# A hybrid decoder layer: transposes of rotated q and k and of gated q and k by VectorE squares and GpSimd transfers

## The chip, the cores and the metric

The kernel runs on one core of a Trainium2 chip. A core has five engines that work side by side, each through its own instructions in order: TensorE (PE; its weight loads are listed apart as PEld), VectorE (DVE), ScalarE (ACT), GpSimd (POOL) and SyncE (SP), which here only issues transfers. They meet through semaphores. Operands lie in SBUF, 128 partitions wide; TensorE writes to PSUM, eight banks of 128 x 512 float32; sixteen DMA engines move data between HBM and SBUF, and from SBUF to SBUF. The metric is the device time of one execution in microseconds (us).

## The reference

One decoder layer over 256 tokens of width 2048, all in float32:

```
x = x + 1/2 * SwiGLU_1(RMSNorm(x))
h = RMSNorm(x);  z = h @ W_in
    group A: 4 heads of chunked gated linear attention (dk 128, dv 256, chunks of 64), low-rank forget gate
    group B: 8 heads of dilated causal attention (d 128), per-head RMS norm of q and k, then rotary
x = x + concat(o_A, o_B) @ W_out
x = x + 1/2 * SwiGLU_2(RMSNorm(x))
```

The change lies in the middle part. In group B, q and k are normed per head, multiplied by the cosines and sines of their position, and then multiplied with each other per head: scores = q k^T, summed over the 128 features of a head. In group A,

```
log_a = log_sigmoid(g_low @ gate_up + bias) / 16
b     = cumsum(log_a) in each chunk of 64
scores  = (q * exp(b - b_ref)) @ (k * exp(b_ref - b))^T
q_inter = q * exp(b);   k_state = k * exp(b_last - b)
```

TensorE sums over the partition dimension. A projection leaves its results with tokens on the partitions and features along the rows, so q and k must be transposed before their scores can be made: to features on the partitions, tokens along the rows.

## The kernel before

**Weights and products.** A large product streams its weights from HBM in 1 MB blocks (raw, three buffers, issued by SyncE). Each half block is split into a high part of reduced precision (wh, ScalarE, line 113) and the rest (wl, VectorE, line 114); both have four buffers. A product of float32 precision is then three matmuls of 128 x 512 (lines 274, 276, 278): high by high, high by low, low by high. `weights()` keeps two pairs prepared beyond the one in use: the split of pair i + 2 is put in the program just before the products of pair i.

**The queue of later work.** `later` is a list of small pieces of work. `column_pair` (line 366) makes 1024 output columns out of 16 pairs, each for two blocks of 128 tokens (t = 0, 1), which gives 32 half-pair steps. Before each step it takes entries from `later`, spread over `span` steps (28 where nothing is said); with `due=i` it empties the list before pair i. An entry `lambda: None` does nothing and spaces the rest out. This fixes the order in the program. The framework then orders each engine's instructions by a simulated timeline, so that what is not ready in the simulation can fall behind what comes later in the program.

**The middle part** (from line 544) runs column pairs one after the other: q of group B (into xq), k of group B (xk), v of group B (va), the low-rank gate (`gate_low`), q and k of group A (qg, kg), v of group A (vg), the output gate, and then the output projection. The work of one column pair's results lies in `later` beside the products of the next.

`rotate` (line 600) handles 128 tokens of four heads of group B: `head_scale` sums squares on ScalarE and takes the power -1/2 on GpSimd (line 165), five VectorE operations scale and rotate (lines 604 to 610) into m1, then four 128 x 128 transposes on TensorE (line 109, through an identity) fill a PSUM bank, and ScalarE copies it into qT or kT (line 614). There are eight such calls, four for q and four for k. `scores` (line 643) multiplies qT by kT, `values` (line 661) applies the probabilities to va. Both put small matmuls among the large ones; all small matmuls share two PSUM banks (tp).

`gate_low` (line 694) has its own weights: two buffers of wh are filled with zeros by GpSimd (line 203) and 16 columns of each k tile are split into them. Two matmuls of the gate's second factor follow (line 708), and for each t ScalarE takes an exponential and a logarithm (lines 712, 713). `decays` (line 718) makes the cumulative sums with TensorE and the exponentials e1, e2, e3. `scaled` (line 734) transposes qg and kg with four TensorE transposes each and VectorE multiplies the bank into e1 and e3, or e2 (line 740). `intra` and `gla_head` make the group's outputs.

**The other way to transpose** is already in the kernel, in the feed-forward parts and in half of the norms: `squares` (line 126) transposes the sixteen 32 x 32 squares of each 128 x 128 block on VectorE, all in place within their 32 partitions, and `move_squares` (line 130) carries the squares to their partitions with 16 GpSimd DMAs, each from 32 partitions to 32 others, in runs of 128 elements (512 bytes). What lands is right up to an order of 32-element runs along the rows; `in_order` and `runs` are views that put this right for the reader.

Tiles of 8 KB per partition in the middle part (xq, qT, xk, kT, va, vg, on, ogh, ogl) share four buffers under the tag `big`.

Of the kernel before, what the change touches and what calls it, by code (L numbers as in the profile page):

```python
# [21 lines left out]
P = 128  # L22
# [5 lines left out]
NT = S // P  # L28
# [20 lines left out]
def layer_kernel(tc, x, xT, gains, gla_gate_up, gla_gate_bias, gla_out_norm, att_q_norm, att_k_norm,  # L49
# [6 lines left out]
    with ExitStack() as es:  # L56
# [69 lines left out]
        def squares(dst, src):  # L126

            nc.vector.transpose(dst.rearrange("p (q j c) -> p j q c", q=4, j=4), src)

        def move_squares(dst, src):  # L130
            for q in range(4):
                for r in range(4):
                    nc.gpsimd.dma_start(dst[32 * q:32 * q + 32, r * P:(r + 1) * P], src[32 * r:32 * r + 32, q * P:(q + 1) * P])  # L133
# [59 lines left out]
        def prepare():  # L193
# [3 lines left out]
            if job == "low":  # L197
# [3 lines left out]
                for i in range(2):  # L201
                    w = wtile("wh").rearrange("p j f -> p (j f)").rearrange("p (k f) -> p k f", f=P)
                    nc.gpsimd.memset(w.bitcast(F32), 0.0)
# [340 lines left out]
        with tc.tile_pool(name="mix", bufs=1, reuse_waits="tile") as mp:  # L544
# [55 lines left out]
            def rotate(i, dst, t, half, xn):  # L600
                rs = head_scale(xn, 4, HD)
# [9 lines left out]
                tb = tp_bank()  # L611
                for h in range(4):
                    transpose(tb[:, h * P:(h + 1) * P], m1[:, h * P:(h + 1) * P])
                nc.scalar.activation(dst[:, 4 * half:4 * half + 4, t * P:(t + 1) * P], v(tb), AF.Copy)

            def store(dst, after=None):

                def f(t, ps):
                    for j in range(2):
                        blk = dst[:, t, j * 512:(j + 1) * 512]  # L620
                        nc.scalar.activation(halves(blk), ps[j], AF.Copy, scale=rt[:, t:t + 1])
                        if after:
                            later.append(lambda blk=blk, j=j: after(t, j, blk))
# [4 lines left out]


            xq, qT = big("xq"), big("qT")  # L630
            qTv = qT.rearrange("p (h s) -> p h s", h=AH)
            column_pair(hacts, store(tok(xq), lambda t, j, b: rotate(0, qTv, t, j, b)), span=14, due=8)
            xk, kT = big("xk"), big("kT")
            kTv = kT.rearrange("p (h s) -> p h s", h=AH)
            column_pair(hacts, store(tok(xk), lambda t, j, b: rotate(1, kTv, t, j, b)))
# [7 lines left out]
            def scores(h):  # L643
                b = tp_bank()
                for t in range(NT):
                    nc.tensor.matmul(b[:, t * P:t * P + (t + 1) * P], lhsT=qTv[:, h, t * P:(t + 1) * P],
                                     rhs=kTv[:, h, :(t + 1) * P], start=True, stop=True)
# [40 lines left out]
            def t4k(name):  # L688
                return mp.tile([P, NT, 512], F32, name=name, tag=name, bufs=1)

            qg, kg, la, e1, e2, e3 = (t4k(n) for n in ("qg", "kg", "la", "e1", "e2", "e3"))
            dec = mp.tile([P, NT, 8], F32, name="dec")

            def gate_low():
# [11 lines left out]
                for t in range(NT):  # L706
                    b = tp_bank()
                    nc.tensor.matmul(b, lhsT=gl[:, t * P:(t + 1) * P], rhs=gup, start=True, stop=True)
                    lg, ab = t512("lg"), t512("ab")
                    nc.vector.scalar_tensor_tensor(lg, b, rt[:, t:t + 1], gbias, op0=ALU.mult, op1=ALU.add)  # L710
                    nc.vector.scalar_tensor_tensor(ab, lg, -1.0, lg, op0=ALU.mult, op1=ALU.min)
                    nc.scalar.activation(ab, ab, AF.Exp)
# [208 lines left out]
```

## Time and profile before

| | |
|---|---|
| time, median of 3 runs (lowest to highest) | 1736.27 us (1733.95 to 1739.5) |
| profiled execution, its time | 1733.12 us |
| profiled execution, span from first to last instruction | 1731.3 us |
| mean granted TensorE clock | 0.999 |
| HBM read, written | 354.57 MB, 4.19 MB |
| rate over the span | 207 GB/s |
| transposes of the kernel on TensorE (line 109) | 120 |
| DMAs of `move_squares` (line 133) | 832 |

The profile is of one execution. A page gives each engine's busy time; the trace behind it can be asked for groups of instructions, single instructions, waits and stretches. A row of the timeline has start, length, engine, line, operation, output <- inputs by the program's names, the shape, a count, and in brackets the idle time of that engine before it with what ended it. A row of a group has a count, the busy time of all, the mean length in ns, and the idle time before them with what ended most of it. The middle part covers about 676 to 1045 us of the span.

### The profile page before, as it was taken

To read this page: it belongs to the slowest core of one execution; us is meant where nothing else is said; L and a number is where in the kernel's file an instruction comes from. 1 tells how busy PE (TensorE), PEld (TensorE's weight loads), DVE (VectorE), ACT (ScalarE), POOL (GpSimd) and SP (SyncE) were. 2 spreads that over 40 slices of the span, in tenths; PEclk is the share of its full clock that TensorE was granted. 3 is DMA by queue.
4 is the path that set the end of the run, shared out by engine and by line. 5 is a ranking of instruction groups with operands and counts; after the bars stand their busy time and mean duration, and the time that the engine had idled before them with its cause. 6 is when DMAs were issued, how large, how long until landed. Compare 5 with 4: busy or idle time off the path is not lost.

```text
span 1731.3 us, 22229 instructions
## 1 busy us (share of the span) xinstructions
PE 1718.3 (99%) x8064; PEld 1498.8 (87%) x8064; DVE 1371.3 (79%) x1643; ACT 940.0 (54%) x1172; POOL 442.4 (26%) x876
## 2 busy tenths in 40 slices
PE   9999999999999999999999998999999999999999
PEld 7888888888888888888888887888888888888887
DVE  6888888888988787566655656788888898897875
ACT  7555555555555555565654544555555555565453
POOL 0333344443400701111000034333333333420000
PEclk9999999999999999999999999999999999999999
DMA  8666566566666666555444466565666655675663
GB/s 342 221 219 229 207 219 221 209 217 233 246 248 218 208 216 239 191 197 216 152 164 170 146 215 222 211 226 208 224 235 226 227 219 208 233 263 209 234 213 137
DMA packets 81710, 373.89 MB, mean 216 GB/s; under 512 B 19344, under 2 KB 36752, under 8 KB 38592
## 3 DMA queue, kind: packets, MB, share of 16 engines
q1 hardware_dynamic: 50864, 350.25, 55.6%
q0 software_dynamic: 30016, 21.16, 4.3%
q8 instruction: 63, 1.03, 0.2%
q10 hardware_dynamic: 720, 1.07, 0.2%
q14 instruction: 47, 0.39, 0.1%
HBM read 354.57 MB, written 4.19 MB: 207 GB/s over the span
## 4 chain that ended last, share of the span: by engine, by line
PE 86%; DVE 6%; DMA 5%; issue 2%; POOL 1%; ACT 1%; DVEq 0%; SPq 0%; ACTq 0%; POOLq 0%
PE acc L276 19%; PE acc L278 19%; PE acc L274 19%; PE tp L278 4%; PE tp L276 4%; PE tp L274 4%; PE acc L299 3%; PE acc L300 3%; PE acc L298 3%; DMA raw<-in_w_ff_dram 2%; DVE wl L114 2%; DMA hh<-us 2%; POOL hh L133 1%; PE tp L298 1%; PE tp L299 1%
## 5 line engine op out<-in xcount | busy, mean ns | idle before, releaser
L114 DVE TENSOR_TENSOR wl<-raw,wh 128x1024 fp32r<-128x1024 f32 (+1 forms) x658 | 790.8, 1217 | 205.8 <-ACT wh L113 201.8
L113 ACT ACTIVATE wh<-raw 128x1024 fp32r<-128x1024 f32 (+1 forms) x660 | 679.0, 1047 | 463.7 <-PE acc L278 205.5
L133 POOL DMA_DIRECT2D xs<-us x704 | 344.3, 497 | 547.5 <-issue 438.4
L276 PE MATMUL acc<-wl,hh 128*128 128x512 f32 x1232 | 372.3, 382 | 0.1
L278 PE MATMUL acc<-wh,hl 128*128 128x512 f32 x1232 | 370.3, 381 | 0.0
L274 PE MATMUL acc<-wh,hh 128*128 128x512 f32 x1232 | 364.8, 382 | 1.8 <-ACT wh L113 1.8
L274 PEld LDWEIGHTS acc<-wh,hh 128*128 128x128 f32 x1232 | 232.6, 190 | 35.4 <-ACT wh L113 2.6
L276 PEld LDWEIGHTS acc<-wl,hh 128*128 128x128 f32 x1232 | 232.9, 190 | 33.8 <-issue 1.0
L278 PEld LDWEIGHTS acc<-wh,hl 128*128 128x128 f32 x1232 | 232.5, 189 | 32.4
L278 PE MATMUL acc<-wh,ul 128*128 128x512 f32 x408 | 123.9, 379 | 0.0
L276 PE MATMUL acc<-wl,uh 128*128 128x512 f32 x408 | 123.9, 379 | 0.0
L274 PE MATMUL acc<-wh,uh 128*128 128x512 f32 x408 | 120.0, 379 | 0.2 <-ACT wh L113 0.2
L133 POOL DMA_DIRECT2D hh<-us x128 | 62.1, 501 | 141.8 <-DVE xs L487 70.5
L274 PEld LDWEIGHTS acc<-wh,uh 128*128 128x128 f32 x408 | 77.1, 189 | 11.4 <-ACT wh L113 0.6
L276 PEld LDWEIGHTS acc<-wl,uh 128*128 128x128 f32 x408 | 77.2, 189 | 10.9
L278 PEld LDWEIGHTS acc<-wh,ul 128*128 128x128 f32 x408 | 77.2, 189 | 10.9
L165 POOL TENSOR_TENSOR rs<-a,mhalf 128x4 f32<-128x4 f32 (+1 forms) x12 | 17.5, 1454 | 256.5 <-DVE a L596 256.5
L238 DVE TENSOR_TENSOR xs<-raw 128x1024 f32<-128x1024 f32 x40 | 48.2, 1206 | 33.5 <-DMA raw<-in_w_ff_dram 33.5
L113 ACT ACTIVATE wh<-xs 128x1024 fp32r<-128x1024 f32 x40 | 42.1, 1054 | 58.7 <-DVE xs L238 51.0
L274 PE MATMUL tp<-wh,hh 128*128 128x512 f32 x240 | 73.2, 379 | 0.0
L276 PE MATMUL tp<-wl,hh 128*128 128x512 f32 x240 | 71.4, 379 | 0.0
L278 PE MATMUL tp<-wh,hl 128*128 128x512 f32 x240 | 71.4, 379 | 0.0
(278 smaller groups left out, 2251.8 us busy)
## 6 DMA issues: line engine op xcount, KB each, us to landing
raw<-in_w_ff_dram SPq DMA_DIRECT2D x175, 1024.0 KB, 5.0
raw<-in_w_dn_dram SPq DMA_DIRECT2D x88, 1024.0 KB, 4.8
raw<-in_w_mix_dram SPq DMA_DIRECT2D x48, 1024.0 KB, 4.7
raw<-in_w_out_dram SPq DMA_DIRECT2D x16, 1024.0 KB, 4.8
xs<-us POOLq DMA_DIRECT2D x704, 16.0 KB, 3.6
xs<-in_x_dram SPq DMA_DIRECT2D x2, 1024.0 KB, 11.0
xs<-in_x_dram POOLq DMA_DIRECT2D x2, 1024.0 KB, 6.3
hh<-us POOLq DMA_DIRECT2D x128, 16.0 KB, 3.6
```

Source lines behind the costliest of these rows:

```text
L113: nc.scalar.activation(dst_h, src, AF.Copy)
L114: nc.vector.tensor_sub(dst_l, src, dst_h.bitcast(F32))
L133: nc.gpsimd.dma_start(dst[32 * q:32 * q + 32, r * P:(r + 1) * P], src[32 * r:32 * r + 32, q * P:(q + 1) * P])
L165: nc.gpsimd.tensor_tensor(dst, src, mhalf[:, :src.shape[-1]], op=ALU.pow)
L238: nc.vector.tensor_add(room["sum"], b1, mid)
L274: nc.tensor.matmul(ps[j], lhsT=sh, rhs=alt(wh[:, j, :]), start=first and i == 0, stop=False)
L276: nc.tensor.matmul(ps[j], lhsT=sh, rhs=alt(wl[:, j, :]), start=False, stop=False)
L278: nc.tensor.matmul(ps[j], lhsT=sl, rhs=alt(wh[:, j, :]), start=False, stop=last and i == len(ws) - 1)
L298: nc.tensor.matmul(bank, lhsT=a[0], rhs=alt(ws[0][:, j, :]), start=start, stop=False)
L299: nc.tensor.matmul(bank, lhsT=a[0], rhs=alt(ws[1][:, j, :]), start=False, stop=False)
L300: nc.tensor.matmul(bank, lhsT=a[1], rhs=alt(ws[0][:, j, :]), start=False, stop=stop)
```

## The change

**Rotated q and k.** `rotate` no longer transposes on TensorE. After the rotation VectorE transposes the squares of m1 into a staging tile (`squares`), and when both halves (four heads each) of a token block are staged, 16 DMAs move them (`move_squares`). The staging tiles are qg and kg for q, la and the third part of e123 for k, all of which get their own contents later. For k the DMAs write kT itself, which now has another order along its rows; `head_runs` gives the score matmul its keys as runs of 32. For q they write the first two thirds of e123, and ScalarE copies them from there into qT in the old order, in four copies of 128 x 512. `move_squares` now carries two halves in one DMA, so each DMA has 32 partitions by 2 x 128 elements, 32 KB, where it had 16 KB.

**Their order.** `head_scale` is an entry of its own in `later`. The rotations are kept back until both token blocks of the column pair have left their banks; then come the four rotations, each with an empty entry behind it, five empty entries, and four entries that take the copies of q.

**Gated q and k.** New tiles `turn` and `moved` (tag `big`) hold the squares of qg and kg before and after the moves, 16 DMAs for each token block. `scaled` multiplies out of `moved` instead of a PSUM bank. In `later`, `turn_qk` comes ahead of `decays`, and each `scaled` has two empty entries before it.

**The gate.** The zeros of its weights are written by VectorE. The exponential and the logarithm run once over both token blocks (128 x 1024) instead of twice (128 x 512). e1, e2 and e3 become parts of one tile, e123.

```diff
-        def squares(dst, src):
+        def squares(dst, src, j=4):
 
-            nc.vector.transpose(dst.rearrange("p (q j c) -> p j q c", q=4, j=4), src)
+            nc.vector.transpose(dst.rearrange("p (q j c) -> p j q c", q=4, j=j), src)
 
         def move_squares(dst, src):
+            n = dst.shape[-1] // 4
             for q in range(4):
                 for r in range(4):
-                    nc.gpsimd.dma_start(dst[32 * q:32 * q + 32, r * P:(r + 1) * P], src[32 * r:32 * r + 32, q * P:(q + 1) * P])
+                    nc.gpsimd.dma_start(dst[32 * q:32 * q + 32, ..., r * n:(r + 1) * n], src[32 * r:32 * r + 32, ..., q * n:(q + 1) * n])
...
-                    nc.gpsimd.memset(w.bitcast(F32), 0.0)
+                    nc.vector.memset(w.bitcast(F32), 0.0)
...
-            def rotate(i, dst, t, half, xn):
-                rs = head_scale(xn, 4, HD)
+            def rotate(i, dst, t, half, xn, rs):
...
-                tb = tp_bank()
-                for h in range(4):
-                    transpose(tb[:, h * P:(h + 1) * P], m1[:, h * P:(h + 1) * P])
-                nc.scalar.activation(dst[:, 4 * half:4 * half + 4, t * P:(t + 1) * P], v(tb), AF.Copy)
+                stage = (qg, kg)[t] if i == 0 else (la, e123[:, 2])[t]
+                squares(stage[:, half, :], m1)
+                if half:
+                    move_squares(dst[:, :, t, :], stage)
+                    if i == 0:
+                        for b in range(2):
+                            copied.append(lambda b=b: nc.scalar.activation(
+                                runs(qTv[:, 4 * b:4 * b + 4, t * P:(t + 1) * P]), in_order(dst[:, b, t, :]), AF.Copy))
+
+            turned, copied = [], []
...
                         if after:
-                            later.append(lambda blk=blk, j=j: after(t, j, blk))
+                            scales = []
+                            later.append(lambda blk=blk, scales=scales: scales.append(head_scale(blk, 4, HD)))
+                            turned.append(lambda blk=blk, j=j, scales=scales: after(t, j, blk, scales[0]))
+                    if after and t:
+                        for f in turned:
+                            later.extend([f, lambda: None])
+                        later.extend([lambda: None] * 5 + [lambda: copied and copied.pop(0)()] * 4)
+                        turned.clear()
...
+            moved_q = e123.rearrange("p e t f -> p (e t f)")[:, :2048].rearrange("p (b t f) -> p b t f", b=2, t=NT)
...
+            kTv = kT.rearrange("p (b t f) -> p b t f", b=2, t=NT)
+
+            def head_runs(a, h, n):
+                return a[:, h // 4, :n, :].rearrange("p t (q j c) -> p (t q) j c", q=4, j=4)[:, :, h % 4, :]
...
-                                     rhs=kTv[:, h, :(t + 1) * P], start=True, stop=True)
+                                     rhs=head_runs(kTv, h, t + 1), start=True, stop=True)
...
-                for t in range(NT):
+                lgs, ab = [t512("lg") for _ in range(NT)], e123[:, 0]
+                for t, lg in enumerate(lgs):
...
-                    lg, ab = t512("lg"), t512("ab")
                     nc.vector.scalar_tensor_tensor(lg, b, rt[:, t:t + 1], gbias, op0=ALU.mult, op1=ALU.add)
-                    nc.vector.scalar_tensor_tensor(ab, lg, -1.0, lg, op0=ALU.mult, op1=ALU.min)
-                    nc.scalar.activation(ab, ab, AF.Exp)
-                    nc.scalar.activation(ab, ab, AF.Ln, bias=1.0)
-                    nc.vector.scalar_tensor_tensor(la[:, t, :], lg, 0.0, ab, op0=ALU.min, op1=ALU.subtract)
+                    nc.vector.scalar_tensor_tensor(ab[:, t, :], lg, -1.0, lg, op0=ALU.mult, op1=ALU.min)
+                nc.scalar.activation(ab, ab, AF.Exp)
+                nc.scalar.activation(ab, ab, AF.Ln, bias=1.0)
+                for t, lg in enumerate(lgs):
+                    nc.vector.scalar_tensor_tensor(la[:, t, :], lg, 0.0, ab[:, t, :], op0=ALU.min, op1=ALU.subtract)
...
             def scaled(t):
-                for src, dsts in ((qg, (e1, e3)), (kg, (e2,))):
-                    tb = tp_bank()
-                    for h in range(GH):
-                        transpose(tb[:, h * P:(h + 1) * P], src[:, t, h * P:(h + 1) * P])
+                for i, dsts in ((0, (e1, e3)), (1, (e2,))):
                     for d in dsts:
-                        nc.vector.tensor_mul(d[:, t, :], tb, d[:, t, :])
+                        d = runs(d[:, t, :].rearrange("p (j q) -> p j q", j=4))
+                        nc.vector.tensor_mul(d, in_order(moved[:, t, i, :]), d)
...
+            turn, moved = (big(n).rearrange("p (t i f) -> p t i f", t=NT, i=2) for n in ("turn", "moved"))
+
+            def turn_qk(t):
+                for i, a in enumerate((qg, kg)):
+                    squares(turn[:, t, i, :], a[:, t, :])
+                move_squares(moved[:, t], turn[:, t])
...
-            for f in (decays, scaled, intra):
+            for f, n in ((turn_qk, 0), (decays, 0), (scaled, 2), (intra, 0)):
                 for t in range(NT):
-                    later.append(lambda f=f, t=t: f(t))
+                    later.extend([lambda: None] * n + [lambda f=f, t=t: f(t)])
```

13 lines of the change are left out of this document (7 added, 6 removed).

## The prediction

> **What bounds the kernel now.** I read the page first, its busy shares.
>
> ```profile
> span 1731.3 us, 22229 instructions
> PE 1718.3 (99%) x8064; PEld 1498.8 (87%) x8064; DVE 1371.3 (79%) x1643; ACT 940.0 (54%) x1172; POOL 442.4 (26%) x876
> ```
>
> TensorE is busy 99% of the span. Since that is a mean over stages, I next asked for sums over the stretches that the edits touch. Columns: stretch, length, busy time of each engine with its instructions, granted clock, DMA share, GB/s.
>
> ```profile
> core 0: us, PE busy (x) PEld busy (x) DVE busy (x) ACT busy (x) POOL busy (x), PEclk, DMA share, GB/s
> 718.00:762.00 44.00, 44.00 (x213) 38.57 (x213) 30.31 (x41) 27.37 (x58) 7.45 (x4) 1.00 0.53 194
> 762.00:805.00 43.00, 43.00 (x209) 37.73 (x208) 27.46 (x41) 24.91 (x56) 10.68 (x9) 1.00 0.58 208
> 861.00:911.00 50.00, 50.00 (x270) 44.37 (x269) 29.49 (x44) 27.92 (x44) 0.00 (x0) 1.00 0.45 156
> 676.00:1045.00 369.00, 369.00 (x1831) 320.47 (x1830) 229.61 (x317) 203.73 (x332) 40.23 (x53) 1.00 0.52 184
> ```
>
> The mixing layer, 676 to 1045 us, has no idle TensorE time at full granted clock, while VectorE is at 62% and ScalarE at 55%. So here one TensorE instruction less is time saved, one more on VectorE, ScalarE or GpSimd is free, and the only way to lose is to make TensorE wait. The last question was what a group of four transposes takes from TensorE: its timeline around the first group.
>
> ```profile
> 731.85 0.59 PE L278 MATMUL acc<-wh,hl 128*128 128x512 f32 x2
> 732.28 0.81 PE L274 MATMUL acc<-wh,hh 128*128 128x512 f32 x3
> ...
> 733.58 0.60 PE L109 MATMUL tp<-ident,m 128*128 128x128 f32 x4
> 733.93 0.46 PE L278 MATMUL acc<-wh,hl 128*128 128x512 f32 x1
> 734.23 0.38 PE L274 MATMUL acc<-wh,hh 128*128 128x512 f32 x1
> ```
>
> Read starts, not durations, because matmuls overlap. Two ordinary matmuls start 0.43 us apart as a pair, 0.216 each. From the first transpose to the second matmul behind the group it is 734.23 - 733.58 = 0.65 us, of which one ordinary matmul is 0.216. A group costs 0.43 us.
>
> **The change part by part.** *Transposes removed.* The rotated blocks (m) and the gated q and k (qg, kg):
>
> ```profile
> L109 PE MATMUL tp<-ident,m x32: 272/273/273, 733.6 to 790.3; 128*128 128x128 f32 x32
> L109 PE MATMUL tp<-ident,qg x8: 272/272/273, 898.4 to 909.3; 128*128 128x128 f32 x8
> L109 PE MATMUL tp<-ident,kg x8: 272/273/273, 903.1 to 909.7; 128*128 128x128 f32 x8
> ```
>
> 32 + 8 + 8 = 48 transposes, twelve groups: 12 x 0.43 = 5.2 us, all inside the stretch without idle time. This is the one term that shortens the chain. The transposes of sc, xs and sg stay.
>
> *Work put on other engines.*
>
> ```profile
> L614 ACT ACTIVATE qT<-tp 128x512 f32<-128x512 f32 x4 | 2.4, 588 | 2.6 <-PE tp L109 2.6
> L614 ACT ACTIVATE kT<-tp 128x512 f32<-128x512 f32 x4 | 2.4, 588 | 2.6 <-PE tp L109 2.6
> L712 ACT ACT_TABLE_LOAD x2 | 2.6, 1283 | 0.0
> L713 ACT ACT_TABLE_LOAD x2 | 2.6, 1283 | 0.0
> L128 DVE STREAM_TRANSPOSE us<-xs 128x512 f32<-128x512 f32 x8 | 5.4, 693 | 0.0
> L153 DVE TENSOR_TENSOR hf<-hh,gT 128x512 f32<-128x512 f32 x2 | 1.4, 684 | 0.0
> L740 DVE TENSOR_TENSOR e<-tp,e 128x512 f32<-128x512 f32 x6 | 3.9, 684 | 2.2 <-PE tp L109 2.2
> L99 DVE MEMSET warm<- 128x512 f32 x1 | 0.5, 485 | 0.1
> L203 POOL MEMSET wh<- 128x1024 f32 x2 | 1.9, 953 | 11.2 <-PE acc L278 11.2
> ```
>
> VectorE gains twelve squares of 0.69 us and two memsets of twice the 0.485 us row: 12 x 0.69 + 2 x 0.97 = 10.3 us, against 369 - 229.6 = 139 us free. The six multiplies of the gated stage read 32-element runs of SBUF instead of a PSUM bank; L153 already reads such runs and takes the same 684 ns, so nothing is added. ScalarE loses eight copies and gets four back (-2.4 us), and two of four table loads go (-2.6 us). Both are costed at nothing: they lie beside TensorE's unbroken work, and without that cover they would be 10.3 us lost and 5 gained. The memset waits, on VectorE as on GpSimd, for a weight buffer that TensorE frees; what queues behind it on VectorE are the splits of later weights, which wait for the same buffers in the same order.
>
> The key operand of the score matmuls becomes runs of 32 elements. All weights are read today in an order that alternates between two halves (alt, line 261), at 0.216 us per 512 columns, so strides as such have no price here: 0, with a loss bounded by the whole of these 32 matmuls (mean 0.33 us, row below), were they to double, less than 10 us; I take that for unlikely.
>
> *Transfers added.* Four moves for rotated blocks and two for the gated ones, each 16 GpSimd DMAs of 32 KB, 64 runs of 512 bytes. The row nearest is the run of 16 KB moves at 566 us; the rope load is the slowest DMA issue.
>
> ```profile
> L133 POOL DMA_DIRECT2D hh<-us x63: 489/492/577, 566.7 to 605.6; - x63
> ...
>   DMA hh<-us: 6.5, 6
>   DVE wl L114: 1.9, 1
> ...
> hh<-us POOLq DMA_DIRECT2D x128, 16.0 KB, 3.6
> L564 POOL DMA_DIRECT2D rope<-in_c_rope_dram x1 | 0.8, 758 | 59.2 <-PE tp L276 59.2
> ```
>
> Call the spacing of two DMAs X. Issue alone gives the lower end, 0.49 us. Start to start with the waits for earlier DMAs, but without the wait for VectorE, gives (605.6 - 566.7 - 1.9) / 63 = 0.59. The upper end is 0.76, the rope issue with its 256 runs. I take 0.59: same operation, same queue, in a burst as here. A move of 16 then takes 9.4 us and lands some 3.6 us later (median time to landing).
>
> *Who waits for them.* ScalarE's four copies of q into qT are the first place. ScalarE works in order, and behind the copies stand the splits of the weights. The clocks of this stage, and the first and last instruction of one rotation:
>
> ```profile
> L621 ACT ACTIVATE xq<-acc,rt x4: 680/686/688, 718.1 to 720.4; 128x512 f32<-128x512 f32 x4
> L621 ACT ACTIVATE xk<-acc,rt x4: 680/688/693, 761.2 to 763.5; 128x512 f32<-128x512 f32 x4
> 741.47 0.69 DVE L604 TENSOR_TENSOR xq<-xq,rs 128x512 f32<-128x512 f32 x1 [0.90 <-POOL rs L165]
> 744.60 0.69 DVE L610 TENSOR_TENSOR m<-m,m 128x512 f32<-128x512 f32 x1
> 796.65 1.23 DVE L114 TENSOR_TENSOR wl<-raw,wh 128x1024 fp32r<-128x1024 f32 x1 [1.36 <-ACT wh L113]
> L646 PE MATMUL tp<-kT,qT x32: 272/328/382, 820.8 to 868.7; 128*128 128x128 f32 x16, 128*128 128x256 f32 x16
> ```
>
> A stage of 16 weight pairs (0 to 15) lasts 761.2 - 718.1 = 43.1 us, 41.3 without its four groups of transposes: 2.58 us per pair. The row at 796.65 is the split of the last pair in the stage after; ScalarE's half of it ends 35.4 us into that stage, 33.7 less four groups, and VectorE's 1.2 later. `later` now holds 21 entries (four scales, four rotations each with an empty entry, five empty, four copies) for 28 half-pair steps, so the second rotation falls in step 9 and the fourth in step 14; a pair's split precedes its steps by two pairs. Step 9 is in pair 4, behind the split of pair 6: 34.9 - 9 x 2.58 = 11.7 us. A rotation takes 3.8 us with a split of 1.2 in it, so 2.6, and a square 0.7. The first move starts at 15.0; the fourth rotation, behind the split of pair 8, ends at 20 us, before the first move does, so the second move lands at 15.0 + 32X + 3.6 = 37.5 us. The third copy stands in step 26, behind the split of pair 14 (33.7 - 2.6 = 31.1 us) and ahead of that of pair 15. In that place ScalarE waits 6.4 us, copies for 0.6, and pair 15 is ready 2.3 us later, at 40.4; TensorE wants it at 15 x 2.58 = 38.7. That is a stall of 1.7 us. But the scheduler orders each engine by simulated readiness: today the first entry of the gated value stage (the cumulative sums) stands at its very start, where the gated q leaves the banks, and runs far behind that place:
>
> ```profile
> L752 ACT ACTIVATE qg<-acc,rq x2: 687/687/687, 858.7 to 860.0; 128x512 f32<-128x512 f32 x2
> L721 PE MATMUL tp<-csq,la x16: 273/275/276, 891.9 to 898.3; 128*128 128x128 f32 x16
> ```
>
> A copy whose transfer is still under way would be put behind the split in the same manner. I take 0 and keep 1.7 for the range.
>
> For k nothing but the scores waits: its transfers land about 37 us after 761.2, at 799, and the first score stands at 820.8. The gate bias load queues behind k's moves on GpSimd, and its reader comes behind the gate matmuls, which end with the row of 816.28 below. For the gated blocks, the tile `moved` gets a buffer that the scores free at 868.7; two moves and a landing end at 868.7 + 32 x 0.59 + 3.6 = 891, and today's first multiply runs here:
>
> ```profile
> 899.03 1.29 DVE L740 TENSOR_TENSOR e<-tp,e 128x512 f32<-128x512 f32 x2 [1.00 <-PE tp L109]
> ```
>
> Eight us to spare. **Sum:** 0 + 0 - 5.2. The profiled execution took 1733.1 us around its span of 1731.3; it would take 1727.9. It stands 3.2 us below the median shown, so the median goes from 1736.3 to 1731.1.
>
> Two rules of the Trainium skill speak against this. "VectorE: DVE Perf Modes", Rules for kernel authors, has a full 128x128 transpose done on TensorE if a PSUM destination will do, since VectorE turns only 32x32 blocks. By that nothing should be gained, 1736.3; the window rows say the opposite for this stage, where TensorE is the one engine without a gap. "SBUF — State Buffer", Who interferes with whom, says that a two-port VectorE operation locks GpSimd out while descriptors are written, which would stretch X; the issue row's spread, 489 to 577 ns beside a busy VectorE, shows 0.09 us of it at most.
>
> **The rivals.** *The copies hold ScalarE (given back).* In the program's place the stall is 15.0 + 32X + 3.6 + 0.6 + 2.3 - 38.7 = 32X - 17.2: 1.7 us at 0.59, and at 0.76 it is 7.1, which eats the gain and 1.9 us more: 1732.8 to 1738.2. For: twice the runs of L133's DMAs. Against: the scheduler, and that the rope load is a first DMA after 59 us of rest.
>
> *The transfers are too slow (slower).* The same place, priced on. To be slower by over 0.3% the stall must be above 5.2 + 5.2 = 10.4 us, hence X above 0.86 us. At X = 1.0, twice the issue row because there are twice the runs, it is 14.8 and the median 1745.9. For: cost in proportion to runs would do exactly that. Against: the rope load has four times these runs and issues in 0.76.
>
> *A little more than the transposes.* PSUM bank rounds fall away too, and the small matmuls may pack closer. Each return from them to the big ones costs extra, as here, and one stage boundary has a wait:
>
> ```profile
> 816.28 0.78 PE L274 MATMUL acc<-wh,hh 128*128 128x512 f32 x1
> 1075.27 1.09 PE L109 MATMUL tp<-ident,xs 128*128 128x128 f32 x4 [4.35 <-DVE hf L123]
> ```
>
> A handful of returns merged (0.78 - 0.38 = 0.4 each, five of them) gives 2 us: 1729. The boundary's wait belongs to the next norm and I see nothing that moves it.
>
> **How the numbers follow.** As summed, no new stall: 0.54, 1731.1. Given back in part or whole: 0.22, about 1735. Slower: 0.12, 1745.9. A little more: 0.12, 1729. The line between faster and no change is 0.3%, 5.2 us, about what a measurement of this kernel can tell, and the forecast lies on it; I put 0.31 of the 0.54 beyond it. Faster 0.31 + 0.12 = 0.43, within 0.23 + 0.22 = 0.45, slower 0.12. The range runs from 1727, the little more less the 2.3 us by which the fastest run shown is below the median, to 1739, the given-back case at its dearest and a little scatter.
>
> **What would show it.** No L109 rows of m, qg, kg, and a mixing layer some 5 us shorter with TensorE still full in every window: the main term. New L133 issues near 0.5 us with starts near 0.59 apart: X. The q copies behind the landing, or ScalarE idle before them without a TensorE gap: the cover. A TensorE gap near the end of the k columns, released by a weight split, shows the first two rivals. Wrong altogether would be longer score matmuls, or a wait of VectorE for `moved` that reaches TensorE.

## The result and the profile after

The changed kernel takes 1725.67 us (median of 5 executions, 1724.26 to 1725.91) against 1736.27 before (also of 5 executions): 0.9944 of the time (95% interval 0.9933 to 0.9954). The forecast was 1731.1, with a range from 1727 to 1739, so the time lies below the range, and the gain of 10.6 us is twice the one forecast. The profiled execution took 1724.26 us, 1.4 below its median. The profile page after, its span and busy shares:

```profile
span 1722.5 us, 22275 instructions
PE 1711.0 (99%) x8016; PEld 1492.5 (87%) x8016; DVE 1379.4 (80%) x1657; ACT 935.1 (54%) x1164; POOL 490.9 (28%) x970
```

TensorE has 48 instructions fewer (8064 to 8016), as the change says. To see where the time went I compare starts: the 7692 matmuls of 128 x 512 of weights stand in the same order in both kernels but for 73 of them, none of these at a stage's end, and the n-th of one is set against the n-th of the other. "Gain" below is how much earlier a stage's end comes, counted from its start.

| stretch, by the clock of before | gain, us | forecast |
|---|---|---|
| start to 676 us (FFN1 and its boundary) | 0.3 | 0 |
| 676 to 1045, the mixing layer | 5.3 | 5.2 |
| 1045 to 1200, the boundary to FFN2 | 3.1 | 0 |
| 1200 to the end, FFN2 | 0.1 | 0 |

So the main term of the forecast came out to the tenth, and 3.1 us came from a place where I had put nothing. These add up to the 8.8 us between the two spans; the rest up to 10.6 is that the profiled execution of before lay 3.2 us below its median, that of after 1.4.

The mixing layer after, in the sums of each engine by stretch (columns as in the prediction):

```profile
740.00:795.00 55.00, 55.00 (x257) 48.19 (x256) 42.69 (x58) 31.84 (x61) 28.88 (x52) 1.00 0.68 231
795.00:874.00 79.00, 79.00 (x403) 69.61 (x402) 51.53 (x87) 47.34 (x77) 11.02 (x21) 1.00 0.58 203
676.00:1039.40 363.40, 363.40 (x1781) 315.38 (x1780) 237.30 (x331) 197.83 (x322) 86.95 (x147) 1.00 0.56 195
```

TensorE is full in every window, as before, but the layer ends at 1039.4 where it ended at 1045. VectorE has 237 us of 363 (62% before, 65% now), GpSimd twice what it had (40 to 87). The transposes that remain on TensorE in the second half are those the prediction said would stay; m, qg and kg are gone:

```profile
L109 PE MATMUL tp<-ident,xs x32: 272/272/273, 681.6 to 1068.2; 128*128 128x128 f32 x32
L109 PE MATMUL tp<-ident,sc x24: 272/273/273, 836.6 to 891.8; 128*128 128x128 f32 x24
L109 PE MATMUL tp<-ident,sg x16: 272/273/329, 968.3 to 983.4; 128*128 128x128 f32 x16
```

Their work is now on VectorE and GpSimd. The new transfers and the gated multiply, in the groups by line:

```profile
L135 POOL DMA_DIRECT2D moved<-turn x32 | 16.9, 534 | 64.5 <-PE tp L674 60.3 <-DMA moved<-turn 4.2
L135 POOL DMA_DIRECT2D e<-qg x16 | 8.5, 540 | 0.6 <-issue 0.6
L135 POOL DMA_DIRECT2D e<-kg x16 | 8.5, 535 | 3.9 <-DMA e<-kg 2.1 <-DMA e<-qg 1.7
L135 POOL DMA_DIRECT2D kT<-e x16 | 8.5, 535 | 8.2 <-DMA kT<-e 3.8 <-issue 2.7 <-DMA kT<-la 1.2
L763 DVE TENSOR_TENSOR e<-moved,e 128x512 f32<-128x512 f32 x6 | 3.9, 688 | 0.2 <-DMA moved<-turn 0.2
```

An issue of 32 KB takes 0.53 to 0.54 us. The multiplies take 688 ns, as out of a PSUM bank, and wait 0.2 us for the moves.

**The boundary.** Half of the norm between the mixing layer and FFN2 is transposed by squares and transfers already in the kernel before. GpSimd's timeline there, and VectorE's multiply that needs the last transfers (hf, line 153), before:

```profile
1047.95 7.76 POOL L133 DMA_DIRECT2D hh<-us  x16 [14.34 <-DVE us L128]
1057.68 4.01 POOL L133 DMA_DIRECT2D hh<-us  x8 [1.97 <-DMA hh<-us]
1062.51 0.49 POOL L133 DMA_DIRECT2D hh<-us  x1 [0.82 <-DMA hh<-us]
1063.53 2.41 POOL L133 DMA_DIRECT2D hh<-us  x5 [0.53 <-DMA hh<-us]
1068.55 0.97 POOL L133 DMA_DIRECT2D hh<-us  x2 [2.62 <-issue]
...
1073.83 0.69 DVE L153 TENSOR_TENSOR hf<-hh,gT 128x512 f32<-128x512 f32 x1 [5.74 <-DMA hh<-us]
```

The last two transfers leave after a pause of 2.62 us in which GpSimd waits for nothing the profile shows. Hence hf comes late, behind it the multiplies that free the banks (line 123), and the four transposes at 1075.27, quoted in the prediction, wait 4.35 us. After, GpSimd, the same multiply (line 155), and the two rows of TensorE that waited:

```profile
1042.35 7.78 POOL L135 DMA_DIRECT2D hh<-us  x16 [13.36 <-DVE us L128]
...
1053.87 3.39 POOL L135 DMA_DIRECT2D hh<-us  x7 [0.50 <-PE tp L109]
1057.69 3.85 POOL L135 DMA_DIRECT2D hh<-us  x8 [0.43 <-DMA hh<-us]
...
1063.83 0.68 DVE L155 TENSOR_TENSOR hf<-hh,gT 128x512 f32<-128x512 f32 x1
...
1056.12 0.70 PE L276 MATMUL acc<-wh,hh 128*128 128x512 f32 x2 [1.21 <-ACT hh L113]
1077.52 0.70 PE L278 MATMUL acc<-wl,hh 128*128 128x512 f32 x2 [1.26 <-DVE wl L114]
```

No pause, no wait of this hf, and 1.21 + 1.26 us of TensorE's time lost where it was 4.35: 1.9 of the 3.1 us. The other 1.2 us fits what the granted clock cost (the figure of each row before DMA share and GB/s). Before, ahead of the wait, in it, and in the stretch in which the clock is low; then after, over the boundary's two short waits and between them:

```profile
1040.00:1070.50 30.50, 30.50 (x146) 26.61 (x146) 19.84 (x25) 14.56 (x21) 16.49 (x34) 1.00 0.64 203
1070.50:1074.50 4.00, 0.42 (x2) 0.02 (x1) 0.67 (x2) 0.00 (x0) 1.23 (x3) 1.00 1.05 430
1074.95:1078.36 3.41, 3.09 (x11) 2.63 (x12) 3.31 (x7) 2.07 (x4) 0.00 (x0) 0.50 0.73 305
```

```profile
1054.00:1062.00 8.00, 6.79 (x32) 5.64 (x31) 4.44 (x5) 4.20 (x5) 7.55 (x16) 1.00 0.48 147
1062.00:1075.00 13.00, 13.00 (x65) 11.40 (x65) 9.08 (x13) 7.76 (x10) 3.42 (x4) 1.00 0.96 325
1075.00:1083.00 8.00, 6.74 (x31) 5.59 (x30) 7.40 (x14) 3.31 (x4) 0.00 (x0) 1.00 0.51 183
```

From 1074.95 us, just before the wait of 4.35 us ends, the granted clock is 0.50 for 3.41 us. TensorE is busy for 3.09 us of that, and half of it, 1.5 us, is an estimate of the most that the clock cost; after the two short waits the clock stays at 1.00. This long wait is paid twice.

### The profile page after: what moved, and what is told of

Same layout as the page of the kernel before. It is cut to its first block, busy times and chain, and to the rows that moved or that the text cites. A ratio compares the mean times of both kernels' runs of the same rounds, so it can differ in the third digit from the quotient of the medians.

```text
span 1722.5 us, 22275 instructions
## 1 busy us (share of the span) xinstructions
PE 1711.0 (99%) x8016; PEld 1492.5 (87%) x8016; DVE 1379.4 (80%) x1657; ACT 935.1 (54%) x1164; POOL 490.9 (28%) x970
## 4 chain that ended last, share of the span: by engine, by line
PE 89%; DVE 4%; DMA 4%; issue 1%; POOL 1%; ACT 1%; DVEq 0%; SPq 0%; ACTq 0%; POOLq 0%
PE acc L278 20%; PE acc L280 20%; PE acc L276 20%; PE tp L280 4%; PE tp L278 4%; PE tp L276 4%; PE acc L301 4%; PE acc L302 4%; PE acc L300 4%; DMA raw<-in_w_ff_dram 2%; DVE wl L114 2%; PE tp L300 1%; PE tp L302 1%; PE tp L301 1%; DMA resid<-xs 1%
## 5 line engine op out<-in xcount | busy, mean ns | idle before, releaser
L135 POOL DMA_DIRECT2D hh<-us x128 | 62.2, 506 | 138.7 <-DVE xs L489 70.8
L113 ACT ACTIVATE swh<-raw 128x512 fp32r<-128x512 f32 x40 | 25.2, 630 | 77.5 <-DMA raw<-in_w_ff_dram 77.5
## 6 DMA issues: line engine op xcount, KB each, us to landing
xs<-in_x_dram SPq DMA_DIRECT2D x2, 1024.0 KB, 10.2
```

The source lines that it names most:

```text
L113: nc.scalar.activation(dst_h, src, AF.Copy)
L135: nc.gpsimd.dma_start(dst[32 * q:32 * q + 32, ..., r * n:(r + 1) * n], src[32 * r:32 * r + 32, ..., q * n:(q + 1) * n])
```

## The experiments

**What the pause hangs on.** In the profiles of all kernels of this case GpSimd stands still for 2.3 to 3.7 us, in most cases released by nothing that the profile shows, each time it has issued 128, 249, 491, 612, 733 or 854 transfers: every 121 (at 370 it waits 1.9 us for VectorE anyway). The kernel before has the boundary's transfers as numbers 430 to 493, so the pause after 491 hits their last burst. The change puts 96 transfers ahead of them; the pause after 491 then falls among k's moves (813 us), and the one after 612 in FFN2 (1112 us). The theory is that this is what moved the boundary. Two kernels shift the count by extra transfers at the start of the mixing layer, so that the pause leaves the last burst (before_pad40) or enters it (after_pad25). The kernel before goes along unchanged, and the changed one with a shift that should do nothing (after_pad12). The edit, with n of 40, 25 and 12:

```diff
             ld(gon, gla_out_norm.unsqueeze(0).to_broadcast([P, GDV]))
+            pad = mp.tile([32, 4 * n], F32, name="pad")
+            [ld(pad[:, 4 * i:4 * i + 4], c_sq[0:32, 4 * i:4 * i + 4]) for i in range(n)]
```

> The kernel of before, unchanged, for a second trace and more times. Theory 1 (GpSimd pauses for some 2.6 us after a fixed count of its DMAs, 128, 249, 370, 491, 612 and so on, 121 apart): the same pause ahead of the third-last... of the last three DMAs of the boundary at 1048 to 1070 us, at the same count of 491, and again over 4 us of TensorE waiting at about 1070 to 1075. Theory 2 (the boundary's wait is drawn anew in each execution by when transfers land): another wait there, anywhere from 1 to 6 us. Ratio to before 1.000 either way.

> Before, with 40 small GpSimd DMAs (32 x 16 bytes) into an unused tile at the start of the mixing layer, where GpSimd idles from 685 to 723 us. Theory 1: the pause after count 491 comes 40 DMAs earlier, in the first burst of moves at about 1015 to 1034 us, where nothing waits; the last burst has no pause, TensorE's wait at the boundary falls from 4.7 us to about 1.5, and the kernel is 2.5 to 3.5 us faster, ratio 0.998 to 0.9985. Theory 2, and theory 3 (the boundary gained because the mixing layer's order or timing changed): ratio 1.000, the boundary as in before.

> The changed kernel with 25 of the same small DMAs at the same place. Theory 1: the pause after count 612 now lies at the same DMA of the boundary's last burst as count 491 did in before; the wait of over 4 us there is back, and 2.5 to 3.5 us of the gain are lost: ratio 0.9960 to 0.9970 against before, where the changed kernel had 0.9944. Theories 2 and 3: nothing changes, 0.9944.

> The control: the changed kernel with 12 small DMAs. All the costs of having such DMAs are here, but the pause after count 612 still lies behind the boundary's last DMA. All theories: 0.9944, the boundary as in the changed kernel. If it is slower like the one with 25, the small DMAs cost by themselves and theory 1 isn't shown by that one.

I measure the boundary as the time between the same two weight matmuls in every kernel, those that start at 1040 and 1110 us in the first profile of before: 70.0 us there, 66.9 after.

Measured: before_again 0.9996 (0.9985 to 1.0007), boundary 70.9. before_pad40 0.9996 (0.9987 to 1.0004), boundary 68.3: the pause moved to 1031.78 us, into the first burst, and the boundary gained, but the whole did not, as FFN1 and FFN2 of this profile were 1.7 us longer. after_pad25 0.9975 (0.9967 to 0.9984), boundary 70.8, with the pause after 612 now in the last burst, the long wait and the low clock back, and a little more lost than expected (the timelines of GpSimd and TensorE, and the sums where the clock is low):

```profile
1065.46 0.98 POOL L135 DMA_DIRECT2D hh<-us  x2 [2.54 <-issue]
...
1072.93 1.09 PE L109 MATMUL tp<-ident,xs 128*128 128x128 f32 x4 [4.16 <-DVE hf L123]
```

```profile
1072.48:1075.89 3.41, 2.96 (x10) 2.52 (x11) 3.33 (x6) 2.20 (x4) 0.00 (x0) 0.50 0.88 370
```

after_pad12 0.9955 (0.9943 to 0.9967), boundary 66.5. Twelve more transfers cost nothing that can be told, thirteen on top of these cost 4.3 us in the boundary and 0.2% of the whole. Nothing else was edited. In the changed kernel the pause decides, then; in the kernel before, its share in the total was not seen.

**The parts alone.** Each part was put into the kernel before by itself: the rotated q and k with their order in `later` (rot_only), the gated q and k (gated_only), and the zeros on VectorE with the one exp and log (gate_only).

gated_only and gate_only against the kernel before:

```diff
-            for f in (decays, scaled, intra):
+            for f, n in ((turn_qk, 0), (decays, 0), (scaled, 2), (intra, 0)):
```

```diff
-                    nc.gpsimd.memset(w.bitcast(F32), 0.0)
+                    nc.vector.memset(w.bitcast(F32), 0.0)
...
+                nc.scalar.activation(ab, ab, AF.Exp)
+                nc.scalar.activation(ab, ab, AF.Ln, bias=1.0)
```

rot_only is the changed kernel with both of these undone.

> Only the rotated q and k go by squares and moves (8 of the 12 groups of transposes); gated q and k, zeros, exponential and logarithm as before. TensorE's work falls by 8 x 0.44 = 3.5 us. Theory 1 (a GpSimd pause every 121 DMAs): 64 DMAs are added, the boundary's last burst has counts 525 to 557, no pause in it, so the 3.1 us at the boundary come too: 6.6 us, ratio 0.9962. Without theory 1: 3.5 us, 0.9980, or with a third of the boundary's gain 4.5.

> Only the gated q and k go by squares and moves (4 groups). TensorE's work falls by 4 x 0.44 = 1.8 us. Theory 1: 32 DMAs are added, the pause after 491 falls at the end of the first burst, where nothing waits, so again the whole 3.1 us at the boundary: 4.9 us, ratio 0.9972. The two parts alone then add up to 11.5 us, 3 more than both together, because each takes the same pause away. Without theory 1 they add up: 1.8 us here, 0.9990.

> Only the zeros by VectorE and one exponential and one logarithm over both token blocks. No DMA is added and no TensorE work falls away: 0, ratio 1.000, with the pause and the wait at the boundary as in before, by every theory.

Measured: gated_only 0.9964 (0.9951 to 0.9976), mixing layer 2.1 us shorter (expected 1.8), boundary 65.7, with the pause in its first burst. gate_only 1.0017 (1.0008 to 1.0026), where 1.000 was expected: mixing layer 0.3 us shorter, the pause in the last burst again and a boundary of 71.2, FFN2 2.5 us longer than in the first profile of before. rot_only came out on the other side, 1.0036 (1.0022 to 1.0049). By 790 us it has gained 3.4 us; then TensorE loses 10.4 up to 840 us. GpSimd's and TensorE's timelines there, and the sums with the clock:

```profile
803.67 3.68 POOL L135 DMA_DIRECT2D kT<-e  x7 [0.49 <-DMA gbias<-in_gla_gate_bias_dram]
809.90 1.06 POOL L135 DMA_DIRECT2D kT<-e  x2 [2.55 <-issue]
810.96 1.86 POOL L205 MEMSET wh<- 128x1024 f32 x2
...
812.65 0.58 PE L723 MATMUL acc<-hh,wh 128*128 128x256 f32 x1 [4.16 <-DVE wh L114]
```

```profile
806.23:816.47 10.24, 6.08 (x22) 4.96 (x23) 1.53 (x3) 0.62 (x3) 4.03 (x7) 0.50 0.53 177
```

The zeros of the low-rank gate's weights, on GpSimd as in the kernel before, stand behind k's 32 transfers and run at 811 us, where before they ran at 798 and 801; behind them wait the split of these weights and TensorE. Ahead of that wait of 4.16 us TensorE has waited 2.08 and 0.77 us for other weight splits, and from 806.23 us, just behind these, its granted clock is 0.50 for 10.24 us. I had not foreseen this. Two kernels test it from both sides, and two more take up what was open: the count of before shifted so far (n = 66, the edit above) that no pause falls into the boundary at all, and the changed kernel with the old gate.

rot_zeros against rot_only (after_zeros_gpsimd is the reverse edit of the changed kernel), and after_old_gate against the changed kernel:

```diff
-                    nc.gpsimd.memset(w.bitcast(F32), 0.0)
+                    nc.vector.memset(w.bitcast(F32), 0.0)
```

```diff
-                lgs, ab = [t512("lg") for _ in range(NT)], e123[:, 0]
-                for t, lg in enumerate(lgs):
+                for t in range(NT):
...
+                    lg, ab = t512("lg"), t512("ab")
...
-                nc.scalar.activation(ab, ab, AF.Exp)
-                nc.scalar.activation(ab, ab, AF.Ln, bias=1.0)
+                    nc.scalar.activation(ab, ab, AF.Exp)
+                    nc.scalar.activation(ab, ab, AF.Ln, bias=1.0)
```

> The rotated q and k by squares and transfers, and the zeros of the low-rank gate's weights on the vector engine; the gated transposes stay on TensorE and the gate has its two exps and two logs. Theory that in rot_only the zeros behind k's 32 transfers in GpSimd's queue were the whole loss: the mixing layer is 3.1 to 3.5 us shorter than before (8 groups of transposes at 0.43 us), nothing is lost between 790 and 835 us, the boundary to FFN2 is 2.5 to 3.6 us shorter since its transfers are numbers 493 to 557, past the pause; ratio 0.9965. Rival, the transfers themselves or the later landing of k hold up the scores or the weights: 5 to 10 us are lost again between 790 and 840 us and the ratio is 1.000 to 1.0035.

> The changed kernel with one line undone: the zeros of the low-rank gate's weights are GpSimd's again. Theory that the zeros queue behind k's transfers: both zeros start only after 811 us instead of 795 and 797 us, TensorE waits 8 to 11 us for the low-rank weights, and the ratio is 1.000 to 1.002, the whole gain gone. Rival, in the changed kernel the planner finds other work for TensorE meanwhile, or puts the zeros ahead of the transfers: a loss under 1 us, ratio 0.9945.

> The changed kernel with the gate's exp and log undone: two exps and two logs of 128 x 512, alternating, with four table loads instead of two. Theory that this part is worth nothing, since TensorE does not wait for the gate: mixing layer 5.3 us shorter than before as in the changed kernel, ratio 0.9945 to 0.995. Rival, the two table loads saved (1.28 us each) reach TensorE: 1 to 2.6 us less gain, ratio 0.9955 to 0.996.

> The kernel before, with 66 more small GpSimd transfers (32 x 16 bytes each, into a buffer that nothing reads) at the start of the mixing layer, where GpSimd stands idle. Its transfers in the boundary between the mixing layer and FFN2 are then numbers 495 to 559, and no multiple of the regularity (128, 249, 370, 491, 612 ...) falls among them: 491 falls among the extra transfers, 612 in FFN2. Theory of the counted pause: the boundary is 2.5 to 3.6 us shorter than in the profile of before, with no pause of 2.3 to 2.9 us in its last burst, and the ratio is about 0.998 (the executions scatter by more than that one by one). Rival, the gain in the boundary comes from something else in the changed kernel (work that comes earlier): the boundary is as long as before within 1 us and the ratio 1.000.

Measured: after_zeros_gpsimd 1.0013 (1.0005 to 1.0022), the whole gain gone by one line (the same two timelines):

```profile
811.44 1.86 POOL L205 MEMSET wh<- 128x1024 f32 x2
...
813.13 0.58 PE L723 MATMUL acc<-hh,wh 128*128 128x256 f32 x1 [4.15 <-DVE wh L114]
```

rot_zeros 0.9978 (0.9968 to 0.9989): nothing lost around 800 us, mixing layer 3.5 us shorter, as expected; but its boundary gained only 0.2 us of the 2.5 to 3.6 expected (below), and 0.9965 was missed. after_old_gate 0.9953 (0.9939 to 0.9966): mixing layer 5.3 us shorter and boundary 66.1, as with the new gate, so the one exp and log are worth nothing that can be told.

before_pad66 missed: 1.0013 (1.0004 to 1.0022). Its boundary is 68.2 us, 1.8 shorter than before where 2.5 to 3.6 were expected, and its mixing layer is 1.2 longer. There the extra transfers have a price of their own: with them the last rotation of q ends only at 769.9 us (745.3 in before), right ahead of those of k, and TensorE waits 0.97 us for a weight split at 774.43. So the total of this run does not tell what the pause is worth. Without the pause the first wait shrinks, but a second one comes up behind it, which the long wait had covered: VectorE splits the next weights only when it is through with sums that overwrite what two residual stores of 1 MB still read. TensorE's timeline in before_pad66; then in rot_zeros, with VectorE's wait for the stores, and the sums behind the second wait:

```profile
1073.62 0.63 PE L109 MATMUL tp<-ident,xs 128*128 128x128 f32 x4 [1.83 <-DVE hf L123]
...
1082.61 0.70 PE L276 MATMUL acc<-wl,hh 128*128 128x512 f32 x2 [1.88 <-DVE wl L114]
```

```profile
1070.85 0.63 PE L109 MATMUL tp<-ident,xs 128*128 128x128 f32 x4 [1.83 <-DVE hf L123]
...
1079.83 0.76 PE L278 MATMUL acc<-wl,hh 128*128 128x512 f32 x2 [1.87 <-DVE wl L114]
...
1077.88 0.76 DVE L318 TENSOR_TENSOR xs<-hh,hl 128x256 f32<-128x256 f32 x2 [1.40 <-DMA resid<-xs]
```

```profile
1080.34:1083.75 3.41, 3.41 (x9) 2.70 (x9) 3.41 (x6) 0.86 (x2) 0.00 (x0) 0.50 0.42 101
```

rot_zeros has no pause in its boundary either and the same two waits, but there the clock falls to 0.50 after the second, and the boundary is 69.8 us. So the theory became: the pause sets the wait, and what the wait costs depends on what is late next and on whether the clock falls.

**The changed kernel again, and the two stores moved.** The last pair asks whether the short boundary is the changed kernel's own, and whether the second wait (1.26 us after) can be had too: the stores are issued from ScalarE's queue, ahead of the norm's last transfers.

```diff
-... nc.gpsimd.dma_start(resid[t * P:(t + 1) * P, :], xs[:, t, :]) ...
+... nc.scalar.dma_start(resid[t * P:(t + 1) * P, :], xs[:, t, :]) ...
```

> The changed kernel again, for a second profile of it. Theory that the boundary to FFN2 gained because no wait of TensorE there is longer than 1.5 us, so that the granted clock stays at 1.00 (with a pause in the last burst the wait is 4.3 us and the clock falls to 0.5 to 0.6 for some 4 us): again no pause in that burst, the boundary 66 to 67 us long between the same two multiplies where before needs 70 to 71, clock 1.00, ratio 0.993 to 0.996. Rival, the short boundary of the first profile was one lucky execution: 68 to 70 us here, and a clock under 1.

> The changed kernel with the two residual stores of 1 MB issued from ScalarE's queue, ahead of GpSimd's last transfers of the norm and not behind them. Theory that the last wait of the boundary (1.26 us, the weights' split on the vector engine behind the sums that overwrite what the stores read) is the stores' landing: the stores are issued earlier, the wait shrinks or goes, boundary 65 to 66 us, ratio 0.993 to 0.9945. Rival, the 2 MB collide with the last transfers of the norm: these land 1 to 3 us later, TensorE waits for them, boundary 67 to 70 us, ratio 0.995 to 0.997.

Measured: after_again 0.9937 (0.9922 to 0.9953), boundary 66.3, waits of 0.64 and 1.21 us in it, clock 1.00 throughout it, so the short boundary was not one lucky execution. after_resid_act 0.9978 (0.9966 to 0.9989), boundary 70.9: a loss somewhat beyond the rival's, and not by the rival's way. The stores go out at 1050 us, and the norm's last transfers do wait 3.66 us for earlier ones to land, but TensorE does not wait for them. With this edit the sums that overwrite what the stores read stand ahead of weight splits that they stood behind in the changed kernel: VectorE waits 4.73 us for the stores to land, ScalarE for VectorE's sums (fh), and the splits of the weights, for which TensorE waits, come behind (timelines of GpSimd, VectorE, ScalarE and TensorE):

```profile
1060.91 3.53 POOL L135 DMA_DIRECT2D hh<-us  x7 [3.66 <-DMA hh<-us]
...
1061.16 0.76 DVE L318 TENSOR_TENSOR xs<-hh,hl 128x256 f32<-128x256 f32 x2 [4.73 <-DMA resid<-xs]
...
1063.01 0.63 ACT L113 ACTIVATE fh<-xs 128x512 fp32r<-128x512 f32 x1 [7.30 <-DVE xs L324]
1063.55 3.88 ACT L113 ACTIVATE wh<-raw 128x1024 fp32r<-128x1024 f32 x4
...
1064.64 0.70 PE L276 MATMUL acc<-wh,hh 128*128 128x512 f32 x2 [3.43 <-ACT wh L113]
```

Of the kernels tried none is faster than the changed one.

| kernel | ratio | mixing layer, us | pause in the boundary | clock falls in the boundary | boundary, us |
|---|---|---|---|---|---|
| before, before_again, gate_only | 1, 0.9996, 1.0017 | 0, 0, -0.3 | last burst | yes | 70.0, 70.9, 71.2 |
| after_pad25 | 0.9975 | -5.3 | last burst | yes | 70.8 |
| before_pad40 | 0.9996 | 0 | first burst | no | 68.3 |
| gated_only | 0.9964 | -2.1 | first burst | no | 65.7 |
| before_pad66 | 1.0013 | +1.2 | none | no | 68.2 |
| rot_only | 1.0036 | +7.6 | none | no | 67.5 |
| rot_zeros | 0.9978 | -3.5 | none | yes | 69.8 |
| after, after_again | 0.9944, 0.9937 | -5.3 | none | no | 66.9, 66.3 |
| after_pad12, after_old_gate | 0.9955, 0.9953 | -5.3 | none | no | 66.5, 66.1 |
| after_zeros_gpsimd | 1.0013 | +5.5 | none | no | 66.5 |
| after_resid_act | 0.9978 | -5.3 | none | yes | 70.9 |

All four boundaries with the pause in the last burst take 70 us or more, and of the others only the two in which the clock falls come near. What stays open: the boundaries with a full clock lie at 67.5 to 68.3 without the gated part and at 65.7 to 66.9 with it. One difference in the traces goes with it. Counted from the boundary's first matmul, VectorE has 12 weight splits ahead of the sums that wait for the stores in every kernel with the gated part (7 in after_resid_act) and 11 in every kernel without. This row of the changed kernel is the twelfth; in before_pad66 the sums come first:

```profile
1070.23 1.22 DVE L114 TENSOR_TENSOR wl<-raw,wh 128x1024 fp32r<-128x1024 f32 x1
...
1075.57 0.76 DVE L318 TENSOR_TENSOR xs<-hh,hl 128x256 f32<-128x256 f32 x2 [3.52 <-DMA resid<-xs]
```

```profile
1080.66 0.76 DVE L316 TENSOR_TENSOR xs<-hh,hl 128x256 f32<-128x256 f32 x2 [1.40 <-DMA resid<-xs]
1081.34 1.22 DVE L114 TENSOR_TENSOR wl<-raw,wh 128x1024 fp32r<-128x1024 f32 x1
```

At a full clock TensorE's waits in the boundary add up to 1.6 to 2.5 us with the twelfth split ahead and to 3.1 to 3.9 without. No run changes this order alone, so that it is the cause is not shown. And FFN2 was 0.6 to 3.2 us longer in all other profiles than in the two first ones, by waits of up to 0.76 us each for weights, as far as they show; which executions have them I could not tie to anything, and it is why the totals of single parts do not add up more closely than some 2 us.

## Why the prediction was wrong, and where it was right

**Main term: right.** Twelve groups at 0.43 us gave 5.2 us; the mixing layer is 5.27 us shorter in both profiles of the changed kernel. The parts agree: 3.5 for the eight rotated groups (3.4 by the same price), 2.1 for the four gated ones (1.7).

**X: inside its bounds for q.** Issue 0.53 to 0.54 us; q's 32 transfers from 740.5 to 761.6 us, 0.66 apart against the 0.59 taken, but they start 7.4 us later than the sum had it (718.1 + 15.0). Twice the runs cost 0.04 us of issue, not twice the issue, so the slower rival had no ground. Of the Trainium skill's lock of GpSimd's descriptor writing beside VectorE, "SBUF — State Buffer", Who interferes with whom, these issues show little: all of q's lie between 533 and 612 ns. VectorE's work beside them was TENSOR_TENSOR and squares, so other operations are not tested. Two small sums of the prediction are off, and nothing hangs on them: VectorE's added work is 10.2 us, not 10.3, and the score matmuls together are 10.5, not under 10.

**The copies of q: right, by the scheduler.** ScalarE's timeline of the copies, and the summary of the score matmuls:

```profile
756.42 1.13 ACT L618 ACTIVATE qT<-e 128x512 f32<-128x512 f32 x2
...
773.51 1.14 ACT L618 ACTIVATE qT<-e 128x512 f32<-128x512 f32 x2
```

```profile
L674 PE MATMUL tp<-kT,qT x32: 272/328/382, 816.9 to 873.9; 128*128 128x128 f32 x16, 128*128 128x256 f32 x16
```

The last two stand 17 us behind the first two, after their transfers have landed, and ScalarE does not wait. In the program's own place, by the prediction's sum, they would have held the splits, which was the given-back rival; no run puts them there. The scores take 272 to 382 ns, as before: runs of 32 elements in the keys cost nothing, as costed.

**k: right in effect, wrong in size.** I had k landing at 799 us, 22 us ahead of its scores. Its moves began at 785.7, 9.5 later than the sum had it (761.2 + 15.0), and the last left only at 814, because of the pause in the middle and waits for earlier landings; the scores began at 816.9. No gap opened, but the slack was all but used up.

**The gated blocks: right.** The multiplies waited 0.2 us.

**The gate: the right number for half of the reason.** "Both are costed at nothing" held for the memset's own time and the table loads. I treated the move of the zeros as a cost to VectorE and never asked what they would meet on GpSimd, though I had put 32 transfers into that queue ahead of them: left there, they cost the mixing layer 10.7 us (-5.3 to +5.5), 7.2 of it waits of TensorE. Without the one edit that I priced as free ballast the whole gain is lost.

**The step that failed:** "The boundary's wait belongs to the next norm and I see nothing that moves it." Two things moved it. The edits issue 96 more GpSimd transfers ahead of it, and the pause that sat in its last burst is tied to their count; and the wait of 4.35 us that hung on that pause also cost clock. Put back into the changed kernel, the pause costs 4.3 us of the boundary and 0.2% of the whole; taken out of the last burst of the kernel before, it gave 1.8 us of the boundary's 3.1 and nothing of the whole. What gives the rest is open; it goes with the gated part and the order on VectorE shown above. The rows for the pause stood in the trace of before, at 128, 249 and 491 transfers; I read the wait from TensorE's side to the multiply that released it, and not on to the transfers and the pause behind them. The boundary's gain was 3.1 us in the first pair of profiles and 4.6 in the second (70.9 to 66.3), which with the main term makes 8.4 to 9.9 of the 10.6. The rival that came nearest in time, "a little more", had another reason, merged returns from the small matmuls; the mixing layer's 5.27 us show nothing of these.

The rule of the Trainium skill on full transposes by TensorE, "VectorE: DVE Perf Modes", Rules for kernel authors, did not hold for this stage, by 5.27 us.

## What to carry to other kernels

Where one engine has no gap, count what each edit takes from it; that number was right. Then follow every queue that is made longer to the instructions behind it, also those that the change happens to move away, and ask of each wait elsewhere what it hangs on, back to the first cause: a wait in a stage that the change does not touch can depend on a count that the change alters. When a wait shrinks, look for the next one behind it and at the granted clock, for here the gain was not the wait's own length.

## What the hardware showed that I had not expected

GpSimd's queue pauses after each 121 of its transfers (128, then 249, 491, 612, 733 and 854; at 370 another wait covers it), whether of 16 or 32 KB or of 512 bytes, for 2.3 to 3.7 us, mostly 2.5 to 2.9. Shifts of the count by 12 to 96 transfers moved the place and not the numbers. What it does in that time the profile does not show.

The granted clock fell to 0.50 in each of the seven profiles in which TensorE waited 3.43 to 4.43 us at a stretch: for 3.41 us in before, 6.8 in before_again, 10.24 in rot_only. "TensorE: Matmul & The Clock Gate" of the Trainium skill, HAM oscillation, has the clock halve after TensorE idles for more than about 3.4 us. The trace agrees for the long waits; but in rot_only the clock had fallen behind waits of 2.08 and 0.77 us, ahead of the long one, and rot_zeros lost its clock after two waits of 1.83 and 1.87 us, while before_pad66, with 1.83 and 1.88, kept it, so short waits near each other can do it too, and it is not sure that they do.
